# Token-major value and output-gate projections, with the lower halves of the weight splits made on GpSimd

## The chip, the cores and the metric

The kernel runs on one core of a Trainium2 chip. The metric is the device time of one execution in microseconds (us); the time given is the median of several executions. The engines are named as in the profile: PE (TensorE), DVE (VectorE), ACT (ScalarE), POOL (GpSimd) and SP (SyncE, which issues most DMAs). Each engine executes its own instructions in a fixed order and waits for others by semaphores.

## The reference

One layer of a hybrid trunk on 2048 latent tokens of width 1024, with 256 context tokens: a gated-linear-attention mixer (GLA, two directions, 4 heads) and a SwiGLU feed-forward network (FFN, width 2816). Only the latent stream is returned.

```python
D_MODEL = 1024; SEQ = 2048; CTX_LEN = 256; GLA_QK = 512; GLA_VD = 1024; GLA_RANK = 16; GLA_CHUNK = 64
mod_l = (silu(c) @ mod_w[i] + mod_b[i]).reshape(bsz, N_MOD, 1, D_MODEL)
h_lat = modulate(rms_norm(lat, norm_g[i, 0]), mod_l[:, 0], mod_l[:, 1])
...
z = h.astype(jnp.float32) @ w_in
q, k, v, r, glr = jnp.split(z, [GLA_QK, 2 * GLA_QK, 2 * GLA_QK + GLA_VD, 2 * GLA_QK + GLA_VD + D_MODEL], axis=-1)
g = log_sigmoid(einsum('blzr,zrk->blzk', glr, w_gate) + b_gate) / GLA_GATE_NORM
...
o_f, s_f = gla_chunk_scan(q, k, v, g_f, s_f0)
o_b, s_b = gla_chunk_scan(flip_seq(q), flip_seq(k), flip_seq(v), flip_seq(g_b), s_b0)
o = head_rms_norm(o_f + flip_seq(o_b), norm_g)
return (o * jax.nn.silu(r)) @ w_out, s_f, s_b
...
lat = lat + mod_l[:, 2] * rms_norm(y_lat, norm_g[i, 1])
h = modulate(rms_norm(lat, norm_g[i, 2]), mod_l[:, 3], mod_l[:, 4])
lat = lat + mod_l[:, 5] * rms_norm(swiglu(h, ffn_w_in[i], ffn_w_out[i]), norm_g[i, 3])
```

## The kernel before

Every large product of fp32 numbers is made of three matmuls of the faster type fp32r: both operands are split into an upper and a lower half, and `mm3` (L86 to L88) adds upper x upper, and upper x lower both ways. For activations and weights, `split` (L73 and L76) makes the upper half with a copy and the lower half with a subtraction on DVE.

The work has stages. First come the modulation vectors and the context tokens (256, to about 84 us in the profile), then four groups of 512 tokens, group 0 to group 3, to about 825 us. For a group, `make_h` transposes the normalised tokens (tp, on PE), scales and shifts them (hf, on ACT, L103) and splits them (hhi, hlo, on DVE), for k = 0 to 7, the eight pieces of 128 input channels. Then units of projection follow. A unit of `col_proj` holds a 128-column block of the weight still and streams 512 tokens: q, k and r. `proj_v` makes 256 columns of v for two tiles of 128 tokens, and `proj_vg` does so for the first 256 columns with the 32 columns of the low-rank gate (glr) behind them; its sums gs go through small DVE instructions and PE transposes (tpg) to glrS. `load_w` loads a weight piece of 128x1024 (wf, two buffers, 512 KB) and splits it into whi (ACT) and wlo (DVE), three buffers each. Projections write to PSUM in the banks pj (two), the transposes of make_h in the banks tp (two).

Between the units stand the stages s0 to s3 of the GLA chunks of 128 tokens of the same group or the one before: gates (pre, gcs, the scan cs), scores (sc, p), transposes of k (kt), the state Tf and the output o. In group 3 the chunk stages start with the 12th unit (`LAST_AT`), and its last three units (`tail`) are kept back. The modulation weights for later stages are summed on DVE (acc, L537) between the units of groups 1 and 2 (`mod_units`).

Phase 2 (860 to 1081 us) goes over the 16 chunks from the last to the first (`back`, b0 to b4): the state E of the backward scan, its output added to op, the norm of each head (on = op times rh), the transposes of on (tp2), the product with silu(r) (rt<-tp, L725), the split into ohi and olo, the output projection py with w_out (wo), the norm and the residual y (on POOL, L754). `load_wo` loads the eight pieces of wo before it, in the transition from 825 to 860 us, through two buffers (wof). Then the FFN follows, first product to 1937 us, second to the end.

The order on each engine is set when the kernel is built, by a scheduler that places instructions by their dependences and estimated times, from the order in which the code is written.

Of the kernel before, what the change touches and what calls it, by code (L numbers as in the profile page):

```python
# [34 lines left out]
def trunk(ctx, tc, x, cx, modw, cols, rows, consts, wqkr, wv, wvg, wgate, wout, w1, w2, out):  # L35
# [10 lines left out]
    r_d = [dram.tile([KT, 128, GT], F32, name=f"r_d{g}") for g in range(NG)]  # L46
# [83 lines left out]
    with tc.tile_pool(name="pro", bufs=1) as pro, tc.tile_pool(name="prop", bufs=1, space=PSUM) as prop:  # L130
# [64 lines left out]
    def make_h(xhs, nt, a):  # L195
# [42 lines left out]
    def col_proj(src, h, n, dst):  # L238
        whi, wlo = load_w(src, "", wp)
        ps = ps1.tile([128, 512], F32, name="pj", tag="pj", bufs=2)  # L240
# [3 lines left out]
        sb = hk.tile([128, GT], F32, name="stg", tag="stg", bufs=2)  # L244
# [23 lines left out]
    turns = []

    def proj_vg(h, g, tp, cache):  # L270
        if 0 not in cache or g == NG - 1:
            cache[0] = [load_vg(wvg[kh]) for kh in range(2)]
        pieces = cache[0]
        i = 1 if g == NG else g % 2
        sb = hk.tile([128, 2, 256], F32, name="stg", tag="stg", bufs=2)
        for t2 in range(2):
            t = 2 * tp + t2
            ps = ps1.tile([128, 512], F32, name="pj", tag="pj", bufs=2)
            for k in range(KT):
                whi, wlo = pieces[k // 4]  # L280
                hhi = h[0][k][:, 128 * t:128 * t + 128]
                hlo = h[1][k][:, 128 * t:128 * t + 128]
                ops = [(320, hhi, whi), (256, hhi, wlo), (288, hlo, whi)]
                if k == KT - 1:
                    ops = ops[1:] + ops[:1]
                for j, (n, a, w) in enumerate(ops):
                    nc.tensor.matmul(out=ps[:, 0:n], lhsT=a, rhs=w[:, k % 4, 0:n], start=(k == 0 and j == 0),  # L287
                                     stop=(k == KT - 1 and j == 2))
            evac(sb[:, t2, :], ps[:, 0:256])
            gs = hk.tile([128, 32], F32, name="gs", tag="gs", bufs=2)  # L290
            nc.vector.tensor_copy(out=gs, in_=ps[:, 288:320])
            nc.vector.tensor_add(out=gs, in0=ps[:, 256:288], in1=gs)  # L292
            nc.vector.tensor_copy(out=glt[2 * (tp % 2) + t2][:, 0:32], in_=gs)
            nc.vector.tensor_copy(out=glt[2 * (tp % 2) + t2][:, 64:96], in_=gs)
            nc.vector.tensor_sub(out=glt[2 * (tp % 2) + t2][:, 32:64], in0=gs, in1=glt[2 * (tp % 2) + t2][:, 0:32].bitcast(F32))
            st.dma_start(out=v_d[g][t, :, 0:256], in_=sb[:, t2, :])

        def turn():
            tps = ps1.tile([128, 512], F32, name="tpg", tag="tp", bufs=2)
            for t2 in range(2):  # L300
                nc.tensor.transpose(out=tps[:, 128 * t2:128 * t2 + 128], in_=glt[2 * (tp % 2) + t2].bitcast(F32), identity=ident)
            nc.vector.tensor_copy(out=glrS[i][:, 256 * tp:256 * tp + 256], in_=tps[:, 0:256])

        turns.append(turn)
# [49 lines left out]
    def gla_stages(g, i, c, first):  # L354
# [58 lines left out]
        def s2():  # L413
# [11 lines left out]
            for z in range(2):  # L425
# [74 lines left out]
    def proj_units(g, h, n):  # L500
# [10 lines left out]
        else:  # L511
# [3 lines left out]
            if g != NG:  # L515
                u += uq
# [710 lines left out]
```

## Time and profile before

| what | us |
| --- | --- |
| median of 3 runs | 2362.84 (2361.79 to 2365.46) |
| profiled execution | 2366.31 |
| its span, first to last instruction | 2364.5 |
| PE busy / DVE / ACT / POOL | 2301.9 / 1566.6 / 1066.5 / 328.4 |
| mean granted clock of TensorE | 0.991 of full speed |

Busy time of an engine is the time in which at least one of its instructions was under way. Matmuls overlap each other, so their mean durations are longer than the distance of their starts. [...] An engine that isn't the bottleneck may stand idle without cost.

### The profile page before, as it was taken

The page shows a single profiled execution, that of the slowest core. Times are in us where ns is not written, and L with a number is a line of the kernel's source. Part 1 is how long each engine was busy: PE and PEld are TensorE (multiplying, and loading weights), DVE is VectorE, ACT ScalarE, POOL GpSimd, SP SyncE. Part 2 cuts the span into 40 slices and gives each one's busy share as a digit, 9 for nine tenths or more (in the row PEclk, how much of TensorE's full clock was granted, in tenths as well). Part 3 has the DMA queues.
Part 4 walks back from the last instruction along what each step waited for, and adds up shares of the span by engine and source line. Part 5 has one row for each costly group of instructions (what it writes and reads, how often), then busy time and mean ns, then how long its engine had stood idle before and what let it go on. Part 6 is the DMA issues. An engine that isn't in the chain of part 4 may idle for free.

```text
span 2364.5 us, 32530 instructions
## 1 busy us (share of the span) xinstructions
PE 2301.9 (97%) x11546; PEld 1940.2 (82%) x11546; DVE 1566.6 (66%) x2462; ACT 1066.5 (45%) x1947; POOL 328.4 (14%) x513
## 2 busy tenths in 40 slices
PE   8999999999998999998999999999999999999998
PEld 4898898898898877776888888888888888888887
DVE  5756767666658586667866666876666657466554
ACT  3525435535546544336333333633333336555552
POOL 1100000000001023643511111111111110011001
PEclk9999999999999999999999999999999999999999
DMA  8765458465455587658633333743344348659655
GB/s 298 224 208 177 141 189 285 167 228 196 160 183 197 191 297 264 227 179 289 227 135 132 129 129 129 245 152 123 127 147 165 134 174 286 195 190 336 195 185 171
DMA packets 213254, 461.36 MB, mean 195 GB/s; under 512 B 22370, under 2 KB 66018, under 8 KB 213092
## 3 DMA queue, kind: packets, MB, share of 16 engines
q1 hardware_dynamic: 195188, 400.56, 50.3%
q0 software_dynamic: 17904, 58.73, 6.8%
q8 instruction: 90, 1.47, 0.3%
q14 instruction: 72, 0.59, 0.1%
HBM read 327.60 MB, written 131.60 MB: 194 GB/s over the span
## 4 chain that ended last, share of the span: by engine, by line
PE 75%; DVE 8%; DMA 6%; issue 5%; POOL 3%; ACT 3%; SPq 0%; POOLq 0%; DVEq 0%; ACTq 0%
PE X L964 19%; PE X L1111 10%; PE Z L964 10%; PE W L1111 8%; PE Y L964 5%; PE pj L87 5%; PE pj L86 5%; PE pj L88 5%; DMA xt<-modw 2%; POOL y L754 1%; PE o L494 1%; DMA xt<-x 1%; DVE cs L335 1%; PE sc L419 1%; PE pj L287 1%
## 5 line engine op out<-in xcount | busy, mean ns | idle before, releaser
L964 PE MATMUL X<-T,whl 128*128 128x512 f32 x2112 | 496.3, 390 | 5.2 <-ACT whl L946 2.1
L964 PEld LDWEIGHTS X<-T,whl 128*128 128x128 f32 x2112 | 397.6, 188 | 89.1 <-ACT whl L946 2.8
L964 PE MATMUL Z<-T,whl 128*128 128x512 f32 x1056 | 254.1, 389 | 1.8 <-ACT whl L946 1.8
L1111 PE MATMUL X<-wr,ar 128*128 128x512 f32 x1056 | 240.9, 389 | 0.0
L964 PEld LDWEIGHTS Z<-T,whl 128*128 128x128 f32 x1056 | 198.2, 188 | 43.2 <-ACT whl L946 2.2
L1111 PEld LDWEIGHTS X<-wr,ar 128*128 128x128 f32 x1056 | 198.2, 188 | 41.5
L86 PE MATMUL pj<-hhi,whi 128*128 128x512 f32 (+1 forms) x544 | 213.4, 395 | 2.1 <-DVE hhi L75 1.4
L87 PE MATMUL pj<-hlo,whi 128*128 128x512 f32 (+1 forms) x544 | 211.1, 388 | 0.0
L88 PE MATMUL pj<-hhi,wlo 128*128 128x512 f32 (+1 forms) x544 | 210.2, 387 | 0.0
L73 ACT CAST whi<-wf 128x1024 fp32r<-128x1024 f32 x104 | 109.0, 1048 | 194.4 <-PE pj L87 83.7
L1065 DVE TENSOR_TENSOR ar<-ar 128x512 fp32r<-128x512 f32 x154 | 106.0, 691 | 128.2 <-ACT ar L1064 127.7
L76 DVE TENSOR_TENSOR wlo<-wf,whi 128x1024 fp32r<-128x1024 f32 x104 | 126.8, 1220 | 87.3 <-ACT whi L73 81.8
L1111 PE MATMUL W<-wr,ar 128*128 128x512 f32 x792 | 180.8, 389 | 0.0
L1111 PEld LDWEIGHTS W<-wr,ar 128*128 128x128 f32 x792 | 148.7, 188 | 31.2
L1064 ACT CAST ar<-ar 128x512 fp32r<-128x512 f32 x154 | 95.5, 622 | 155.3 <-DMA ar<-S_d 120.1
L86 PE MATMUL pj<-whi,hhi 128*128 128x256 f32 x432 | 125.6, 291 | 5.9 <-DVE gs L292 4.9
L947 DVE TENSOR_TENSOR whl<-s,whl 128x512 fp32r<-128x512 f32 x132 | 98.2, 746 | 47.3 <-ACT whl L946 46.5
L964 PE MATMUL Y<-T,whl 128*128 128x512 f32 x528 | 127.6, 390 | 0.0
L87 PE MATMUL pj<-wlo,hhi 128*128 128x256 f32 x432 | 124.0, 287 | 2.9 <-DVE wlo L76 2.9
L88 PE MATMUL pj<-whi,hlo 128*128 128x256 f32 x432 | 123.4, 286 | 0.0
L87 PEld LDWEIGHTS pj<-hlo,whi 128*128 128x128 f32 x544 | 103.5, 190 | 21.2 <-DVE hlo L76 2.2
L86 PEld LDWEIGHTS pj<-hhi,whi 128*128 128x128 f32 x544 | 103.0, 190 | 21.4 <-DVE hhi L75 1.6
(234 smaller groups left out, 4428.6 us busy)
## 6 DMA issues: line engine op xcount, KB each, us to landing
ar<-S_d SPq DMA_DIRECT2D x154, 256.0 KB, 2.8
wf<-wqkr SPq DMA_DIRECT2D x68, 512.0 KB, 4.1
wg<-w SPq DMA_DIRECT2D x44, 512.0 KB, 3.8
wu<-w SPq DMA_DIRECT2D x88, 256.0 KB, 3.0
S_d<-sa POOLq DMA_DIRECT2D x88, 256.0 KB, 2.3
wr<-W_d SPq DMA_DIRECT2D x88, 256.0 KB, 2.9
wf<-wv SPq DMA_DIRECT2D x36, 512.0 KB, 4.0
S_d<-a POOLq DMA_DIRECT2D x66, 256.0 KB, 3.3
```

The lines of the kernel that those rows point to most:

```text
L73: nc.scalar.copy(out=hi, in_=src)
L76: nc.vector.tensor_sub(out=lo, in0=src, in1=hi.bitcast(F32))
L86: nc.tensor.matmul(out=ps, lhsT=ahi, rhs=bhi, start=start, stop=False)
L87: nc.tensor.matmul(out=ps, lhsT=ahi, rhs=blo, start=False, stop=False)
L88: nc.tensor.matmul(out=ps, lhsT=alo, rhs=bhi, start=False, stop=stop)
L287: nc.tensor.matmul(out=ps[:, 0:n], lhsT=a, rhs=w[:, k % 4, 0:n], start=(k == 0 and j == 0), stop=(k == KT - 1 and j == 2))
L335: nc.vector.tensor_tensor_scan(out=flat(cs[:, 4 * hh:4 * hh + 4, :]), data0=flat(rst), data1=flat(gcs), initial=0.0, op0=ALU.mult, op1=ALU ...
L947: nc.vector.tensor_sub(out=w[:, 1, :], in0=src, in1=w[:, 0, :].bitcast(F32))
L964: nc.tensor.matmul(out=ps, lhsT=w[:, a, ks], rhs=t[:, k, b, :], start=first and k == 0 and n == 0, stop=k == 3 and n == 2, skip_group_chec ...
L1064: nc.scalar.copy(out=t[:, 0, :], in_=raw)
L1065: nc.vector.tensor_sub(out=t[:, 1, :], in0=raw, in1=t[:, 0, :].bitcast(F32))
L1111: nc.tensor.matmul(out=po[j], lhsT=a[:, x, 128 * j:128 * j + 128], rhs=w[:, z, :], start=first and fp == 0 and n == 0, stop=fp == NFP - 1 ...
```

## The change

Projections: v and r are now made by `token_units`: for up to four tiles of 128 tokens a half of 512 columns at a time, each tile in a PSUM bank of its own, from four pieces of weight (each two k times 512 columns). In the context and in group 3 two tiles at a time. r is stored by token and no longer transposed. `proj_vg` is replaced by `glr_unit`: 16 matmuls against the gate's columns, a copy on ACT, six small DMAs that repeat the rows, and three DVE instructions. A piece's lower half is made by POOL, not by DVE. The number of pieces goes from 104 and 12 with the gate's columns to 124.

PSUM: four banks pj serve the units, make_h and the sums of mod_units; the buffers stg are four instead of two. A last sum of mod_units waits while a token unit has its banks open.

Order: make_h of group 0 stands behind all units of the context. In group 3 the gates of the first direction of chunks 0 and 1 are made two units and one unit ahead of `LAST_AT`. A kt that nobody used (second direction, chunk 0 of each sequence) is left out. The last three r units come ahead of all loads of wo.

Phase 2: silu(r) is multiplied in together with the head norm, before the transposes; ohi is a copy on ACT from PSUM, olo a subtraction on DVE that reads PSUM; the head norm's gain is multiplied into wo.

```diff
+    def load_w(src):
+        w = wp.tile([128, D], F32, name="wf", tag="wf", bufs=2)
         sync.dma_start(out=w, in_=src)
...
+        hi = wp.tile([128, D], F32R, name="whi", tag="whi", bufs=3)
+        lo = wp.tile([128, D], F32R, name="wlo", tag="wlo", bufs=3)
+        nc.scalar.copy(out=hi, in_=w)
+        nc.gpsimd.tensor_tensor(out=lo, in0=w, in1=hi.bitcast(F32), op=ALU.subtract)
         return hi, lo
...
+    def token_units(g, h, c, tiles, dst):
+
+        ps = []
+        step = 1 if len(tiles) == 4 else 2
+
+        def unit(p0):
+            held[0] = p0 + step < 4
+            if p0 == 0:
+                ps.extend(ps1.tile([128, 512], F32, name="pj", tag="pj", bufs=4) for t in tiles)
+            for p in range(p0, p0 + step):
+                whi, wlo = load_w(wvr[c, p])
+                for j, t in enumerate(tiles):
+                    for k2 in range(2):
+                        k, ks, ts = 2 * p + k2, slice(512 * k2, 512 * k2 + 512), slice(128 * t, 128 * t + 128)
+                        mm3(ps[j], h[0][k][:, ts], h[1][k][:, ts], whi[:, ks], wlo[:, ks], k == 0, k == KT - 1)
+                    if p == 3:
+                        sb = hk.tile([128, GT], F32, name="stg", tag="stg", bufs=4)
+                        evac(sb, ps[j])
+                        st.dma_start(out=dst(t), in_=sb)
...
+    def glr_unit(g, h, n):
         i = 1 if g == NG else g % 2
...
+        ps = ps1.tile([128, 512], F32, name="pj", tag="pj", bufs=4)
+        for k in range(KT):
+            nc.tensor.matmul(out=ps[0:64, 0:n], lhsT=wgs[:, k, :], rhs=h[0][k][:, 0:n], start=k == 0, stop=False,
+                             skip_group_check=True)
+            nc.tensor.matmul(out=ps[0:32, 0:n], lhsT=wgs[:, k, 0:32], rhs=h[1][k][:, 0:n], start=False, stop=k == KT - 1,
+                             skip_group_check=True)
+        g2, m, c = (hk.tile([128, GT], F32, name=x, tag="stg", bufs=4) for x in ("g2", "gm", "gc"))
+        nc.scalar.copy(out=g2[0:64, 0:n], in_=ps[0:64, 0:n])
+        for j in range(3):
+            sync.dma_start(out=m[32 * j:32 * j + 32, 0:n], in_=g2[0:32, 0:n])
+            sync.dma_start(out=c[32 * j:32 * j + 32, 0:n], in_=g2[32:64, 0:n])
+        nc.vector.tensor_add(out=m[0:96, 0:n], in0=m[0:96, 0:n], in1=c[0:96, 0:n])
+        nc.vector.tensor_copy(out=glrS[i][0:96, 0:n], in_=m[0:96, 0:n])
+        nc.vector.tensor_sub(out=glrS[i][32:64, 0:n], in0=m[32:64, 0:n], in1=glrS[i][32:64, 0:n].bitcast(F32))
...
-            transp_mod(ps1, "tp", 2, xhs, k, hf[:, 0:n], mcol[:, a, 1, k:k + 1], mcol[:, a, 0, k:k + 1])
+            transp_mod(ps1, "pj", 4, xhs, k, hf[:, 0:n], mcol[:, a, 1, k:k + 1], mcol[:, a, 0, k:k + 1])
...
+            v = [w for tp in range(2) for c in range(2) for w in v_units(c, (2 * tp, 2 * tp + 1))]
+            r = [w for tp in (1, 0) for c in (2, 3) for w in r_units(c, (2 * tp, 2 * tp + 1))]
...
-            hn = [make_h(norm_rows(x[0:GT, :], 4), 4, 0)]
...
+            xh0 = norm_rows(x[0:GT, :], 4)
             load_consts()
         u()
+    hn = [make_h(xh0, 4, 0)]
...
+                else:
+                    if stages:
+                        stages.pop(0)()
+                    if i + 1 in (LAST_AT - 2, LAST_AT - 1):
+                        gates(g, 0, i + 3 - LAST_AT)
...
-            split(w, *wo[k])
+            g = col[:, 96 + k % 2:97 + k % 2]
+            nc.scalar.activation(out=wo[k][0], in_=w, func=AF.Copy, scale=g)
+            nc.vector.scalar_tensor_tensor(out=wo[k][1], in0=w, scalar=g, in1=wo[k][0].bitcast(F32),
+                                           op0=ALU.mult, op1=ALU.subtract)
...
-                nc.vector.tensor_scalar_mul(out=on[:, h, :], in0=op[:, h, :], scalar1=rs[:, h:h + 1])
+                nc.vector.scalar_tensor_tensor(out=on[:, h, :], in0=op[:, h, :], scalar=rs[:, h:h + 1], in1=e["rt"][:, h, :],
+                                               op0=ALU.mult, op1=ALU.mult)
...
-                split(rt[:, ks, :], ohi[:, ks, :], olo[:, ks, :], "dve")
+                split(tp, ohi[:, ks, :], olo[:, ks, :])
```

What the edits move is seen in the order of the engines. On PE, the end of the context units, where make_h of group 0 (tp<-ident,xh, four transposes for each k) begins. Before, one k at a time between matmuls of the context's v:

```order
L88 MATMUL pj<-whi,hlo 128x256
L102 MATMUL tp<-ident,xh 128x128 x4
L86 MATMUL pj<-whi,hhi 128x256
L87 MATMUL pj<-wlo,hhi 128x256
L102 MATMUL tp<-ident,xh 128x128 x4
L88 MATMUL pj<-whi,hlo 128x256
```

Now all context units are done when it comes, and the first matmuls of group 0 (pj<-hhi,whi) stand right behind it; the gates of the first context chunk (pre) fall between the last of the transposes:

```order
L87 MATMUL pj<-wlo,hhi 128x512
L88 MATMUL pj<-whi,hlo 128x512
L102 MATMUL tp<-ident,xh 128x128 x20
L302 MATMUL pre<-glrS_377,wg_380 128x256 x2
L102 MATMUL tp<-ident,xh 128x128 x4
L302 MATMUL pre<-glrS_377,wg_380 128x256 x2
L302 MATMUL pre<-glrS_377,wg_381 128x256 x4
L102 MATMUL tp<-ident,xh 128x128 x8
L86 MATMUL pj<-hhi,whi 128x512
L87 MATMUL pj<-hlo,whi 128x512
```

The eight k have moved out of the cover of the context's matmuls. On POOL, the first chunk's copies of the scan (lnDf, lnDb) and the small steps of the norms (ma, ra). Before:

```order
L80 TENSOR_SCALAR ma<-ss 128x1
L82 TENSOR_TENSOR ra<-ma,nhalf 128x1
L342 COPY lnDf<-mid 128x4x2
L343 COPY lnDf<-cs_1046 128x4x2
L80 TENSOR_SCALAR ma<-ss 128x1
L82 TENSOR_TENSOR ra<-ma,nhalf 128x1
L342 COPY lnDb<-mid 128x4x2
L343 COPY lnDb<-cs_1070 128x4x2
L342 COPY lnDf<-mid 128x4x2
L343 COPY lnDf<-cs_1986 128x4x2
```

Now the splits of the weight pieces (wlo) stand in the same queue:

```order
L82 TENSOR_TENSOR ra<-ma,nhalf 128x1
L219 TENSOR_TENSOR wlo<-wf,whi 128x1024
L80 TENSOR_SCALAR ma<-ss 128x1
L82 TENSOR_TENSOR ra<-ma,nhalf 128x1
L318 COPY lnDb<-mid 128x4x2
L319 COPY lnDb<-cs_991 128x4x2
L80 TENSOR_SCALAR ma<-ss 128x1
L82 TENSOR_TENSOR ra<-ma,nhalf 128x1
L219 TENSOR_TENSOR wlo<-wf,whi 128x1024 x14
L318 COPY lnDf<-mid 128x4x2
L219 TENSOR_TENSOR wlo<-wf,whi 128x1024
L319 COPY lnDf<-cs_1699 128x4x2
```

A copy or a norm's step on POOL now waits for the splits ahead of it. On SP, the loads of wo (wof) and what is stored and loaded around them before:

```order
L672 DMA op_8331<-op_d_144 128x1024
L646 DMA wof<-wout 128x1024 x2
L660 DMA rt<-r_d_77 128x4x128
L246 DMA r_d_77<-stg 128x512
L668 DMA ub_8426<-ub_d_159 128x1024
L646 DMA wof<-wout 128x1024 x2
L670 DMA qb_8428<-qb_d_175 128x512
L672 DMA op_8430<-op_d_143 128x1024
```

And after:

```order
L641 DMA rt<-r_d_88 128x1024
L215 DMA wf<-wvr 128x1024
L628 DMA wof<-wout 128x1024 x2
L650 DMA ub_7656<-ub_d_170 128x1024
L652 DMA qb_7658<-qb_d_186 128x512
L654 DMA op_7660<-op_d_154 128x1024
L628 DMA wof<-wout 128x1024
L261 DMA r_d_86<-stg 128x512
L261 DMA r_d_87<-stg 128x512
L628 DMA wof<-wout 128x1024
```

The last weight piece of a projection (wf) now stands ahead of the first wof, and the stores of r from the last unit behind the third.

## Rows read from the trace of the kernel before

**Rows 1.** The page: the chain of waits that ended last.

```profile
PE 75%; DVE 8%; DMA 6%; issue 5%; POOL 3%; ACT 3%; SPq 0%; POOLq 0%; DVEq 0%; ACTq 0%
```

**Rows 2.** Windows by stage: length, busy time of each engine (instructions), clock, DMA.

```profile
35.00:84.00 49.00, 44.91 (x333) 42.79 (x333) 33.44 (x67) 24.38 (x35) 2.53 (x6) 0.94 0.69 223
...
620.00:825.00 205.00, 196.86 (x1233) 178.79 (x1232) 135.75 (x214) 115.83 (x208) 9.75 (x10) 0.98 0.52 180
...
860.00:1081.00 221.00, 210.26 (x993) 171.04 (x992) 145.76 (x276) 90.21 (x236) 102.96 (x130) 0.98 0.69 233
1081.00:1937.00 856.00, 846.94 (x3730) 700.31 (x3729) 595.75 (x902) 343.32 (x603) 144.45 (x242) 0.99 0.47 160
1937.00:2364.50 427.50, 420.26 (x1852) 347.13 (x1850) 252.23 (x374) 210.88 (x387) 26.39 (x53) 1.00 0.66 222
```

**Rows 3.** Waits of PE, projections: for whom, us in total, times, longest.

```profile
PE tp L102 <- ACT hf L103: 6.6, 6, 2.8
PE pj L86 <- DVE gs L292: 4.9, 2, 4.3
PE pj L87 <- DVE wlo L76: 2.9, 3, 2.1
...
PE pj L287 <- DVE whig L212: 2.4, 2, 1.4
```

**Rows 4.** Waits of PE, phase 2.

```profile
PE o L696 <- ACT hf L103: 3.9, 2, 3.2
...
PE tp L723 <- DVE on L704: 2.5, 1, 2.5
```

**Rows 5.** Windows at the start of group 3.

```profile
720.00:724.30 4.30, 0.00 (x0) 0.03 (x1) 4.28 (x8) 4.12 (x7) 1.27 (x2) 0.91 0.34 122
724.30:734.00 9.70, 8.40 (x37) 7.77 (x38) 9.70 (x24) 3.92 (x9) 1.96 (x2) 0.51 0.25 79
```

**Rows 6.** Timeline of PE at two places: start, length, instruction.

```profile
160.49 0.28 PE L88 MATMUL pj<-whi,hlo 128*128 128x256 f32 x1
160.61 0.28 PE L86 MATMUL pj<-whi,hhi 128*128 128x256 f32 x1
...
1117.40 2.88 PE L964 MATMUL Z<-T,whl 128*128 128x512 f32 x12
```

**Rows 7.** Groups of DVE instructions, 0 to 825 us: busy, mean ns, idle before.

```profile
L76 DVE TENSOR_TENSOR wlo<-wf,whi 128x1024 fp32r<-128x1024 f32 x104 | 126.8, 1220 | 87.3 <-ACT whi L73 81.8 <-PE sc L419 4.2 <-PE pj L548 1.2
...
L211 DVE TENSOR_TENSOR wlog<-wfg,whig 128x1024 fp32r<-128x1024 f32 x12 | 14.7, 1222 | 3.6 <-ACT whig L210 3.5
```

**Rows 8.** Single lines: count, ns shortest/median/longest, starts, form.

```profile
L754 POOL TENSOR_TENSOR y<-y,xt x15: 2338/2390/2792, 864.7 to 1077.8; 128x1024 f32<-128x1024 f32 x15
...
L75 DVE CAST ohi<-rt x32: 412/417/1659, 834.2 to 1066.3; 128x512 fp32r<-128x512 f32 x32
...
L684 DVE SCALAR_TENSOR_TENSOR E<-E,fb,ub x60: 467/475/2614, 819.2 to 1011.6; 128x256 f32<-128x256 f32 x60
...
L704 DVE TENSOR_SCALAR on<-op,rh x64: 341/349/2494, 827.9 to 1057.3; 128x256 f32<-128x256 f32 x64
...
L725 DVE SCALAR_TENSOR_TENSOR rt<-tp,col,rt x64: 469/475/484, 832.3 to 1065.3; 128x256 f32<-128x256 f32 x64
...
L342 POOL COPY lnDf<-mid x9: 194/1131/3481, 99.9 to 748.5; 128x8 f32<-128x8 f32 x9
```

**Rows 9.** The page's DMA issues (us to landing), and whi's line.

```profile
wf<-wqkr SPq DMA_DIRECT2D x68, 512.0 KB, 4.1
...
L73 ACT CAST whi<-wf x104: 1029/1049/1062, 28.5 to 807.1; 128x1024 fp32r<-128x1024 f32 x104
```

**Rows 10.** make_h: hf's line, and PE's timeline in group 2.

```profile
L103 ACT ACTIVATE hf<-tp,mcol x72: 547/775/797, 34.3 to 1101.7; 128x512 f32<-128x512 f32 x64, 128x256 f32<-128x256 f32 x8
...
432.59 0.66 PE L102 MATMUL tp<-ident,xh 128*128 128x128 f32 x4 [2.23 <-ACT hf L103]
```

**Rows 11.** The last wo_lo, from its line.

```profile
L76 DVE TENSOR_TENSOR wo_lo<-wof,wo_hi x8: 1211/1216/1226, 825.5 to 858.1; 128x1024 fp32r<-128x1024 f32 x8
```

More of the change, by code (lines that the diff above doesn't have):

```diff
@@ L34, in trunk @@
 @with_exitstack
-def trunk(ctx, tc, x, cx, modw, cols, rows, consts, wqkr, wv, wvg, wgate, wout, w1, w2, out):
+def trunk(ctx, tc, x, cx, modw, cols, rows, consts, wqk, wvr, wgl, wgate, wout, w1, w2, out):
     nc = tc.nc
@@ L45, in trunk @@
     v_d = [dram.tile([4, 128, D], F32, name=f"v_d{g}") for g in range(NG + 1)]
-    r_d = [dram.tile([KT, 128, GT], F32, name=f"r_d{g}") for g in range(NG)]
+    r_d = [dram.tile([128, D], F32, name=f"r_d{c}") for c in range(NC_)]
     T_d = [[dram.tile([4, 128, GT], F32, name=f"T_d{p}{i}") for i in range(7)] for p in range(2)]
@@ L238, in col_proj @@
     def col_proj(src, h, n, dst):
-        whi, wlo = load_w(src, "", wp)
-        ps = ps1.tile([128, 512], F32, name="pj", tag="pj", bufs=2)
+        whi, wlo = load_w(src)
+        ps = ps1.tile([128, 512], F32, name="pj", tag="pj", bufs=4)
         for k in range(KT):
@@ L268, in trunk @@
[L268 to L273, printed above, removed]
-        i = 1 if g == NG else g % 2
[L275 to L304, printed above, removed]
@@ new lines, in trunk @@
+    held = [False]
+    def token_units(g, h, c, tiles, dst):
[12 more added lines that the diff above has]
+                    if p == 3:
+                        sb = hk.tile([128, GT], F32, name="stg", tag="stg", bufs=4)
+                        evac(sb, ps[j])
+                        st.dma_start(out=dst(t), in_=sb)
+        return [lambda p0=p0: unit(p0) for p0 in range(0, 4, step)]
@@ L424, in s2 @@
             e["kt"] = []
-            for z in range(2):
+            for z in range(2 if gc else 1):
                 kt = gtile([128, H, 128], "kt")
@@ L443, in s3 @@
             vhi, vlo = e["vhi"], e["vlo"]
-            for z in range(2):
+            for z in range(len(e["kt"])):
                 khi, klo = e["kt"][z]
-                if z == 1 and gc == 0:
-                    break
                 if z == 1 and not (is_ctx and c == 0):
@@ L554, in finish @@
             else:
[L555 removed]
+                ps = ps1.tile([128, KT, 2], F32, name="pj", tag="pj", bufs=4)
                 for k in range(KT):
@@ L605, in trunk @@
                 extra[i]()
-            if mu and i >= 1:
-                mu.pop(0)()
+            if mu and i >= 1 and not (mu[0][0] and held[0]):
+                mu.pop(0)[1]()
             if is_last:
@@ L802, in trunk @@
     bk[0][0]()
-    load_wo(range(0, 4), c2, c2)
-    bk[0][5]((0,))
     tail[0]()
@@ L807, in trunk @@
     bk[1][0]()
-    bk[1][5]((0,))
     tail[1]()
-    bk[0][2]((0,))
     bk[1][1]()
-    for u in tail[2:]:
-        u()
-    bk[0][5]((1,))
-    bk[1][5]((1,))
+    tail[2]()
+    load_wo(range(0, 4), c2, c2)
     bk[2][0]()
```

152 lines of the change are left out of this document (52 added, 100 removed).

## The prediction

> **What bounds the kernel now.** I read the chain of waits first, then the busy time by stage, then what TensorE (PE) waited for in each stage. The chain is 75% PE [rows 1], so time is lost or won only where PE stands still or has more to do. The two FFN stages take 856 + 427.5 = 1283.5 us [rows 2]; the change edits no instruction in them, and I carry them over. What can move lies in the first 1081 us.
>
> There the waits of PE are few. In the projections it waited 6.6 us for hf (the scaled transposes in make_h), 4.9 us for gs (the gate sums of proj_vg), 2.9 us for wlo and 2.4 us for whig [rows 3]; in phase 2 it waited 3.9 us for hf and 2.5 us for on [rows 4]. [...]
>
> **The change part by part.**
>
> *Matmuls.* Two matmuls of 256 columns start 0.12 us apart, so two take 0.24 us; twelve of 512 columns took 2.88 us, the last one's 0.39 us included, which is (2.88 - 0.39) / 11 = 0.226 us each [rows 6]. The change removes 1296 matmuls of 256 (155.5 us) and 432 of proj_vg (256, 288 and 320 columns; at 0.13 us, a little over the 256's, 56.2 us), and adds 864 of 512 (195.3 us), 64 glr matmuls of 512 columns and 16 of 256 (16.4 us together); 18 transposes and 4 kt transposes go (an estimate of 0.1 us each, 2 us). Sum: **-2 us**. r keeps 768 matmuls of 512 columns, with the operands exchanged. The durations in the busy lists would tell another story, since matmuls overlap; the starts decide.
>
> *The splits on DVE.* 104 wlo splits of 1.22 us (126.8 us) and 12 wlog (14.7 us) leave DVE [rows 7], and with them the waits for wlo and whig, 2.9 + 2.4 us, and the lower clock behind the largest one (2.1 of the 2.9 us), which I put at 1 to 2 us: **-5 us** (0 to -7). Nothing is gained where DVE was only busy.
>
> *The splits on POOL.* The trace has no such instruction of POOL before 860 us. The nearest is the addition y of 128x1024 in phase 2: 2.34 to 2.79 us, median 2.39 [rows 8]; I take 2.4 us, and 124 of them are 298 us in some 790. What it does to DVE is the question. ohi takes 0.417 us and up to 1.66, E 0.475 and up to 2.61, on 0.349 and up to 2.49 [rows 8]: the long ones lie beside such a POOL instruction and end with it. Copies that read PSUM, rt<-tp, stay at 0.469 to 0.484 [rows 8]. The lock works the other way too: POOL's lnDf copy takes 0.19 us at best, 1.13 at the median and 3.48 at most [rows 8]. So each split holds up any DVE instruction that has all its inputs in SBUF. In the projections these are about 314 (36 scans, 28 acc, 36 ek, 32 eq, 40 hhi, 40 hlo, 18 vlo and others, counted from the program). POOL holds the lock 298/790 = 38% of the time; a DVE instruction that meets it waits half of 2.4 us: 314 x 0.38 x 1.2 = 143 us of DVE, an estimate, and as much as the 141.5 us taken away. DVE is then as late as before, at other places. The lower bound is no delay, if POOL waits instead; the upper one is all 143 us on DVE. PE feels little of that: before, with DVE as busy, it waited 10 us for it in the whole of [rows 3]. I take **+3 us** (0 to +12).
>
> [...]
>
> *Supply of pieces.* wf has two buffers. One turns over in landing (4.1 us), upper half on ACT (1.05) and lower half: 1.22 us on DVE before, 2.39 after [rows 7 to 9]. With about 0.5 us between steps that is 6.9 and 8.1 us for two pieces, 3.4 and 4.1 us each. A piece feeds 24 matmuls of 0.227 = 5.4 us in groups 0 to 2: no loss. In ctx and group 3 it feeds 12, 2.7 us. Group 3 has 8 pieces of 5.4 and 32 of 2.7, 131 us, in the 205 us from 620 to 825: 5.1 us a piece if the chunk work were spread evenly, which hides 4.1. It isn't: the last six pieces have none (at most 6 x 1.4 = 8 us). I take **+6 us** (0 to +15). In ctx 12 pieces need 12 x 4.1 = 49 us where they needed 41, which is why make_h of group 0 could hide between them; now it stands behind them. Its transposes then go at ACT's pace, 0.775 us for hf against 4 x 0.11 on PE [rows 10]: 8 x 0.33 = 2.7 us and the first wait. The stage lasted 49 us before; I take **+2 us** (-4 to +8).
>
> *make_h of groups 1 to 3.* All 8 k stand ahead of the first matmuls, in the same four banks as these. Group 2 did almost so before and waited 2.23 us there [rows 10], within the 6.6. I charge **+5 us** for three (0 to +9).
>
> *Start of group 3.* The gs that PE waited for at 720 stood on DVE behind four gate groups in a row. glr_unit makes no gs, and two of the gate groups now come one and two units earlier. [...] I take **-6 us** (0 to -9).
>
> *Transition.* The last r pieces come ahead of all wo loads. The first can be issued one turn of wf's buffers before the projections end at 825 [rows 2], near 820, and eight pieces in two buffers take four turns of 6.9 us (priced as wf before): the last is split near 848. The last wo_lo started at 858.1 before [rows 11]. So the loads are hardly later than they were; the first w_out matmuls are, and are covered by less: **+3 us** (0 to +6).
>
> *Phase 2.* Each chunk loses four rt<-tp (0.475) and two ohi (0.417 to 1.66) on DVE, and on turns into an instruction with two inputs (like E, 0.475). DVE's chain from the transposes to olo gets 2 to 3 us shorter, and two instructions less can meet POOL's y; ACT gets two casts (1.05 us for 1024 columns, so some 0.6 each). PE waited 2.5 + 3.9 us here [rows 4], with lower clock behind each; on itself is still held by y. **-5 us** (0 to -9).
>
> The rest I cost at nothing: the norm's gain in the wo splits (the same two instructions a piece, on the same engines), four stg buffers, r stored and loaded by chunk (as many bytes), and mod's last sums held while a token unit has its banks (two units at most, with nothing behind them before group 3). The cover of the last is the chunk work; without it they would cost the length of a unit once, some 5 us.
>
> Sum: -2 - 5 + 3 + 6 + 2 + 5 - 6 + 3 - 5 = +1 us on the span of 2364.5, in an execution of 2366.31 us. That execution lies 3.5 us above the median of 2362.84, so I forecast 2362.84 + 1 = **2364 us**.
>
> **The rivals.**
>
> *A, what I forecast:* the parts cancel. Its own range is -8 to +10 us, 2355 to 2373.
>
> *B, faster:* the waits of PE that DVE made go, and POOL's lock falls into time in which PE doesn't need DVE. Then -2 (matmuls) - 9 (start of group 3) - 7 (wlo and whig) - 9 (phase 2) + 2 (make_h) = -25 us, 2338. For it: in groups 0 to 2 PE waits for DVE so seldom that DVE has slack. Against it: ctx and group 3 have none.
>
> *C, slower:* the lock holds up POOL's splits themselves. DVE's longer instructions take 1.2 us; if one stands ahead of each split, a piece takes 4.1 + 0.6 = 4.7 us with two buffers. In group 3 that is 32 x (4.7 - 4.1) = 19 us, in ctx 12 x (4.7 - 3.4) = 16 us, less the 7 us of wlo and whig: +28 us, with half a clock behind each stall rather more, 2391. It decides as soon as a piece takes longer to make than the work that it feeds. The 3.48 us copy [rows 8] speaks for it; that a split waits ahead of time, with three buffers of whi and wlo, against it. [...]
>
> **How the numbers follow.** About 0.2% (4.7 us) is what can be told from no change. I give A 0.42, B 0.25 and C 0.33. Of A's range some two thirds lie within 4.7 us: same 0.27, and 0.07 faster and 0.08 slower. So faster 0.32, same 0.27, slower 0.41. The range goes to half of B and nearly to C: 2346 to 2388.
>
> **What the profile will show.** Right: POOL's splits at 2.4 us or more, and DVE's SBUF instructions (E, on; hlo, ek, eq and acc in the projections) with means above their undisturbed times; in the waits of PE, wlo comes back under POOL's name, in ctx and group 3, and gs and whig are gone; phase 2 is shorter than the 221 us of [rows 2]. Wrong: if PE doesn't wait for POOL at all (then B), if it waits in groups 0 to 2 (worse than C), if the stretch from 718 us on loses its lower clock entirely, or if the FFN stages change, which I held fixed.

## The result, and the profile after

The changed kernel takes 2407.39 us (median of 4 executions, 2403.67 to 2412.85) against 2364.15 us of the kernel before, run beside it: a ratio of 1.0172, 95% interval 1.0154 to 1.0190. It is 43 us slower. The forecast was 2364 us with a range of 2346 to 2388. "Slower" had the largest of the three chances, but the size and the mechanism were missed.

The head of the page after (span; busy us and share of the span of each engine):

```profile
span 2411.1 us, 30732 instructions
...
PE 2316.1 (96%) x10740; PEld 1908.4 (79%) x10740; DVE 1500.1 (62%) x2149; ACT 1090.0 (45%) x1984; POOL 628.3 (26%) x637
```

The windows of the changed kernel by stage: the context, groups 0, 1, 2, group 3 to the last projection, phase 2, and the first FFN product (length, busy time of each engine, clock, DMA):

```profile
35.00:95.00 60.00, 48.42 (x252) 40.09 (x252) 30.08 (x44) 26.05 (x37) 34.24 (x21) 0.87 0.65 205
95.00:257.00 162.00, 156.01 (x720) 129.06 (x721) 90.68 (x108) 71.99 (x115) 67.91 (x40) 0.96 0.54 180
257.00:448.00 191.00, 181.68 (x933) 153.11 (x932) 110.23 (x138) 90.13 (x157) 68.26 (x42) 0.99 0.57 190
448.00:640.00 192.00, 183.53 (x937) 154.83 (x937) 122.02 (x144) 89.93 (x154) 69.29 (x41) 0.98 0.62 206
640.00:886.00 246.00, 219.72 (x1149) 186.88 (x1148) 152.10 (x194) 135.30 (x238) 103.85 (x52) 0.94 0.56 191
886.00:1125.00 239.00, 231.64 (x1092) 188.22 (x1091) 127.39 (x220) 114.57 (x284) 104.70 (x132) 0.99 0.70 247
1125.00:1983.00 858.00, 846.27 (x3727) 699.64 (x3726) 596.71 (x898) 341.97 (x599) 144.69 (x242) 0.99 0.46 158
```

The kernel before took 49 us for the first of these [rows 2] and, from the same view of its trace, 158, 186 and 185 us for groups 0 to 2, and 220 + 249 = 469 us from there to the FFN:

```profile
84.00:242.00 158.00, 154.00 (x914) 137.61 (x913) 103.61 (x156) 73.89 (x119) 14.01 (x17) 0.99 0.59 196
242.00:428.00 186.00, 181.51 (x1116) 161.62 (x1115) 126.37 (x188) 88.16 (x153) 7.74 (x16) 1.00 0.65 216
428.00:613.00 185.00, 182.08 (x1116) 163.04 (x1115) 121.61 (x187) 88.53 (x154) 11.60 (x18) 0.99 0.56 190
```

After, it is 60, 162, 191, 192 and 246 + 239 = 485 us: 11, 4, 5, 7 and 16 us more. The loss lies in every stage of the projections. The FFN's first product takes 858 us against 856 [rows 2]; POOL's busy time in each of the groups 0 to 2 went from between 8 and 14 us to 68 or 69.

What PE waited for from 35 to 886 us (us in total, times, longest), the view of [rows 3]:

```profile
PE o L86 <- DVE Tf L435: 14.4, 5, 3.3
PE pj L87 <- POOL wlo L219: 11.9, 7, 5.3
PE tp L102 <- ACT hf L103: 8.4, 6, 2.0
PE pj L86 <- DVE stg L229: 5.7, 2, 4.2
PE pj L86 <- ACT hf L103: 4.4, 4, 2.3
...
PE U L86 <- DVE gcs L309: 3.8, 2, 2.2
PE U L86 <- DVE Tf L435: 2.8, 2, 1.5
```

The sums of proj_vg (gs, whig) are gone, as they must be; in their place PE waits for Tf, for wlo under POOL's name, and longer for hf and for copies of projections (stg). Before, it waited 2.7 us in all for Tf:

```profile
PE o L86 <- DVE Tf L461: 2.7, 2, 1.7
```

The places differ. In groups 0 to 2 PE waits for nothing that POOL makes, and 18.8 us for DVE; its 11.9 us for wlo lie in the context (4.6) and in group 3 (7.3). POOL's split is what it was priced at (ns shortest, median, longest):

```profile
L219 POOL TENSOR_TENSOR wlo<-wf,whi x124: 2345/2398/3591, 29.7 to 878.9; 128x1024 fp32r<-128x1024 f32 x124
```

DVE's instructions with two inputs in SBUF, in the projections (busy us, mean ns, idle before):

```profile
L311 DVE TENSOR_TENSOR_SCAN cs<-rst,gcs 128x516 f32<-128x516 f32 x36 | 54.4, 1511 | 0.9
...
L370 DVE SCALAR_TENSOR_TENSOR eq<-qc,eq 128x512 f32<-128x512 f32 x32 | 35.2, 1101 | 8.3 <-ACT eq L366 6.5 <-DMA qc<-q_d 1.8
...
L377 DVE TENSOR_TENSOR fz<-lnDf 128x4 f32<-128x4 f32 x17 | 20.1, 1183 | 4.4 <-POOL lnDf L319 2.9 <-ACT ts L416 0.9
...
L76 DVE TENSOR_TENSOR plo<-p,phi 128x512 fp32r<-128x512 f32 x16 | 15.3, 956 | 0.1
```

In the kernel before they took 1.23, 0.68, 0.16 and 0.68 us on the mean. One of the five waits for Tf, near the end of group 2, in the timelines of DVE, POOL and PE:

```profile
612.26 2.88 DVE L76 TENSOR_TENSOR plo<-p,phi 128x512 fp32r<-128x512 f32 x1
615.06 1.27 DVE L435 TENSOR_TENSOR Tf<-ts,U 128x512 f32<-128x512 f32 x2
```

```profile
612.21 2.38 POOL L219 TENSOR_TENSOR wlo<-wf,whi 128x1024 fp32r<-128x1024 f32 x1 [3.76 <-ACT whi L218]
```

```profile
613.60 0.28 PE L88 MATMUL U<-vhi,klo 128*128 128x256 f32 x1
615.79 0.48 PE L86 MATMUL o<-vhi,phi 128*128 128x256 f32 x1 [1.92 <-DVE Tf L435]
```

plo was ready to go at 612.26, 0.05 us after a split on POOL; it ends only at 615.14, half a microsecond behind the split, instead of at 612.94. Tf stands behind it on DVE, and PE's next matmuls need the PSUM bank that Tf reads: 1.92 us of nothing. And behind the stall the clock falls, as it did at the start of group 3 before [rows 5]:

```profile
615.70:622.00 6.30, 6.21 (x26) 5.53 (x27) 1.13 (x3) 2.16 (x4) 0.00 (x0) 0.73 0.52 163
```

0.73 of full speed on the mean of 6.3 us (0.50 in the windows of half a microsecond from 616.2 to 619.2 us, 1.00 in those from 619.7) is, as an estimate, another 6.3 x 0.27 = 1.7 us. The mean granted clock of the whole execution went from 0.991 to 0.982.

### The profile page after: what moved, and what is told of

It reads as the page before. It is cut to its first block, busy times and chain, and to the rows that moved or that the text cites. A ratio compares the mean times of both kernels' runs of the same rounds, so it can differ in the third digit from the quotient of the medians.

```text
span 2411.1 us, 30732 instructions
## 1 busy us (share of the span) xinstructions
PE 2316.1 (96%) x10740; PEld 1908.4 (79%) x10740; DVE 1500.1 (62%) x2149; ACT 1090.0 (45%) x1984; POOL 628.3 (26%) x637
## 4 chain that ended last, share of the span: by engine, by line
PE 52%; DMA 1%; DVE 1%; POOL 1%; ACT 1%; issue 1%; SPq 0%; POOLq 0%; ACTq 0%; DVEq 0%
PE X L934 19%; PE X L1081 10%; PE Z L934 9%; PE W L1081 7%; PE Y L934 5%; DMA T<-T_d 0%; POOL y L730 0%; DMA T_d<-hf 0%; DMA wg<-w 0%; DVE whl L917 0%; PE tp L102 0%; PE py L87 0%; PE py L86 0%; PE py L88 0%; DMA rt<-r_d 0%
## 5 line engine op out<-in xcount | busy, mean ns | idle before, releaser
L219 POOL TENSOR_TENSOR wlo<-wf,whi 128x1024 fp32r<-128x1024 f32 x124 | 308.3, 2488 | 403.9 <-ACT whi L218 389.9
L218 ACT CAST whi<-wf 128x1024 fp32r<-128x1024 f32 x124 | 129.9, 1048 | 223.4 <-PE pj L88 64.2
L87 PE MATMUL pj<-wlo,hhi 128*128 128x512 f32 x544 | 216.1, 397 | 11.9 <-POOL wlo L219 11.9
L86 PE MATMUL pj<-whi,hhi 128*128 128x512 f32 x544 | 218.8, 403 | 6.5 <-DVE stg L229 5.7
L88 PE MATMUL pj<-whi,hlo 128*128 128x512 f32 x544 | 215.3, 396 | 0.0
L962 POOL DMA_DIRECT2D S_d<-a x66 | 35.6, 540 | 458.1 <-DVE a L952 364.7
L87 PEld LDWEIGHTS pj<-wlo,hhi 128*128 128x128 f32 x544 | 104.2, 192 | 36.4 <-POOL wlo L219 15.4
L86 PEld LDWEIGHTS pj<-whi,hhi 128*128 128x128 f32 x544 | 104.0, 191 | 30.1 <-DVE stg L229 6.6
L88 PEld LDWEIGHTS pj<-whi,hlo 128*128 128x128 f32 x544 | 104.2, 191 | 22.2
L86 PE MATMUL pj<-hhi,whi 128*128 128x512 f32 (+1 forms) x288 | 112.4, 395 | 4.4 <-ACT hf L103 4.4
```

Of the source, the lines that this page charges most:

```text
L86: nc.tensor.matmul(out=ps, lhsT=ahi, rhs=bhi, start=start, stop=False)
L87: nc.tensor.matmul(out=ps, lhsT=ahi, rhs=blo, start=False, stop=False)
L88: nc.tensor.matmul(out=ps, lhsT=alo, rhs=bhi, start=False, stop=stop)
L218: nc.scalar.copy(out=hi, in_=w)
L219: nc.gpsimd.tensor_tensor(out=lo, in0=w, in1=hi.bitcast(F32), op=ALU.subtract)
L962: nc.gpsimd.dma_start(out=S_d[self.p][i][self.f % NFP], in_=t)
```

## The experiments

Each run was compared with the kernel before on the same chip; all ratios are to that kernel. "DVE's splits" below is the first run. Port theory, supply theory and structure theory are the three explanations that its expectation names. No run shows a port; what is meant, and what the runs can show, is that POOL's splits hold up DVE's instructions with SBUF inputs.

**The splits back on DVE**, all else as changed.

```diff
-        nc.gpsimd.tensor_tensor(out=lo, in0=w, in1=hi.bitcast(F32), op=ALU.subtract)
+        nc.vector.tensor_sub(out=lo, in0=w, in1=hi.bitcast(F32))
```

> The changed kernel with the lower halves of the weight pieces made on DVE again, all else as changed. Port theory (POOL's splits hold up DVE's instructions with SBUF inputs, and PE waits for Tf, eq and the scans): most of the 43 us come back, 2355 to 2375 us, and PE's wait for Tf falls from 14 us to under 5. Supply theory (a piece takes longer to make, so wf turns over more slowly): comes back too, 2360 to 2375, and above all in the context and in group 3. Structure theory (token units, make_h in one piece, banks and order cost the time, whoever makes the splits): stays at 2390 or above.

Measured: 2350.3 us, ratio 0.9928 (0.9904 to 0.9951). All of the loss came back and more: without POOL's splits the change is 18 us faster than the kernel before beside it (2368.48 us). The windows by stage (context, groups 0, 1, 2, group 3, phase 2), and PE's waits in the projections:

```profile
35.00:86.00 51.00, 45.20 (x253) 38.54 (x253) 32.72 (x57) 25.59 (x38) 2.85 (x6) 0.91 0.72 239
86.00:240.00 154.00, 151.82 (x720) 125.21 (x721) 101.06 (x133) 72.04 (x114) 17.25 (x18) 1.00 0.57 191
240.00:420.00 180.00, 179.14 (x935) 152.03 (x934) 117.25 (x159) 90.68 (x157) 11.99 (x16) 1.00 0.60 203
420.00:600.50 180.50, 178.96 (x932) 151.87 (x932) 124.37 (x168) 89.35 (x153) 10.64 (x16) 1.00 0.65 218
600.50:824.00 223.50, 213.68 (x1154) 182.54 (x1153) 160.37 (x232) 135.98 (x238) 11.28 (x14) 0.98 0.60 209
824.00:1068.00 244.00, 232.74 (x1090) 187.96 (x1088) 127.13 (x222) 115.34 (x285) 105.90 (x132) 0.99 0.68 242
```

```profile
PE tp L102 <- ACT hf L103: 3.4, 3, 1.9
PE pj L86 <- ACT hf L103: 2.8, 5, 1.0
PE pj L87 <- DVE wlo L219: 2.3, 5, 0.7
PE o L86 <- DVE Tf L435: 1.7, 2, 1.1
...
PE U L86 <- DVE Tf L435: 1.3, 1, 1.3
```

Structure theory falls. Port and supply theory both fit; the next runs part them.

**POOL busy for nobody, with DVE's splits.** For each piece POOL subtracts the upper half from itself, in two instructions of 128x512, into a scratch tile that nobody reads.

```diff
+        nc.vector.tensor_sub(out=lo, in0=w, in1=hi.bitcast(F32))
+        dm = wp.tile([128, 512], mybir.dt.bfloat16, name="dm", tag="dm", bufs=1)
+        for j in range(2):
+            hj = hi[:, 512 * j:512 * j + 512].bitcast(F32)
+            nc.gpsimd.tensor_tensor(out=dm, in0=hj, in1=hj, op=ALU.subtract)
```

> [...] Port theory: as slow as the changed kernel or slower, since DVE has its splits too: 2400 to 2430 us. Supply theory: as fast as with DVE's splits alone, within 6 us.

Measured: 2407.76 us, ratio 1.0170 (1.0150 to 1.0190): as slow as the change, though nothing reads POOL's result. DVE's own splits (1.22 us undisturbed) and scans (1.23) are held up, and PE waits for Tf again:

```profile
L219 DVE TENSOR_TENSOR wlo<-wf,whi 128x1024 fp32r<-128x1024 f32 x124 | 175.1, 1412 | 91.5 <-ACT whi L218 91.3
L315 DVE TENSOR_TENSOR_SCAN cs<-rst,gcs 128x516 f32<-128x516 f32 x36 | 49.4, 1371 | 0.6
```

```profile
PE o L86 <- DVE Tf L439: 11.0, 5, 3.5
...
PE pj L87 <- DVE wlo L219: 8.9, 10, 2.8
```

So the loss comes with POOL's instructions, whoever makes the pieces. The run doesn't free the pieces of POOL entirely: before it fills a buffer of whi again, ACT must wait until POOL has read it, and PE waited 2.6 us for whi and 8.9 us for DVE's wlo.

**Half of each split on POOL.**

```diff
+        nc.vector.tensor_sub(out=lo[:, 0:512], in0=w[:, 0:512], in1=hi[:, 0:512].bitcast(F32))
+        nc.gpsimd.tensor_tensor(out=lo[:, 512:1024], in0=w[:, 512:1024], in1=hi[:, 512:1024].bitcast(F32), op=ALU.subtract)
```

> The changed kernel with half of each lower half (512 columns) on DVE and the other half on POOL. [...] Port theory: half of the loss stays, 2380 to 2395 us. Supply theory: nearly all comes back, 2360 to 2372 us.

Measured: 2381.34 us, ratio 1.0059 (1.0040 to 1.0078). 31 of the 57 us between the change and DVE's splits remain: about half, as the port theory had it. The supply isn't quite restored here, though: POOL's half took 1.66 us on the mean, more than half of the change's 2.49, and PE waited 6.5 us for wlo (11.9 in the change, 2.3 with DVE's splits). By itself this run doesn't part the two theories.

**POOL's splits in the kernel before.**

```diff
-        split(w, hi, lo)
+        nc.scalar.copy(out=hi, in_=w)
+        nc.gpsimd.tensor_tensor(out=lo, in0=w, in1=hi.bitcast(F32), op=ALU.subtract)
```

> The kernel before, with its 104 wlo splits (not the 12 with the gate's columns) made by POOL, and nothing else changed. Port theory: slower by 20 to 45 us, 2385 to 2410, with PE waiting for Tf. Supply theory: slower by 5 to 20 us, in the context and in group 3. Structure theory: no change, within 5 us of 2364.

Measured: 2413.31 us, ratio 1.0193 (1.0170 to 1.0216), 45 us slower, a little over the range; PE waited 15.0 us for Tf. The one edit costs as much in the old structure as the whole change cost.

**A busy POOL that hardly reads.**

```diff
+        nc.vector.tensor_sub(out=lo, in0=w, in1=hi.bitcast(F32))
+        dm = wp.tile([128, 256], F32, name="dm", tag="dm", bufs=1)
+        nc.gpsimd.tensor_copy(out=dm[:, 0:1], in_=hi[:, 0:1].bitcast(F32))
+        for j in range(6):
+            nc.gpsimd.memset(dm, 0.0)
```

> As the run with DVE's splits, and for each piece POOL copies one column of the upper half (so that it comes at the piece's pace) and then fills a scratch tile of 128x256 six times, about as long as a split: POOL is as busy, but hardly reads SBUF. [...] If any busy POOL disturbs the others (its queue, power, writes): 2385 to 2410 us.

Measured: 2359.37 us, ratio 0.9967 (0.9954 to 0.9980), well below the 2385 of a POOL that disturbs merely by being busy. POOL was busy for more time than the change's 308 us of splits, and yet 48 of the 57 us are not there; DVE's instructions with two inputs in SBUF have their undisturbed means (casts and others with one input are a little longer: hhi 448 ns against 421):

```profile
L223 POOL MEMSET dm<- 128x256 f32 x744 | 238.2, 320 | 42.1
L221 POOL COPY dm<-whi 128x1 f32<-128x1 f32 x124 | 97.1, 783 | 313.6 <-ACT whi L218 311.6
```

```profile
L315 DVE TENSOR_TENSOR_SCAN cs<-rst,gcs 128x516 f32<-128x516 f32 x36 | 44.2, 1228 | 0.6
...
L374 DVE SCALAR_TENSOR_TENSOR eq<-qc,eq 128x512 f32<-128x512 f32 x32 | 21.9, 683 | 1.5 <-ACT khi L73 0.9 <-DMA qc<-q_d 0.5
```

So it is POOL's reading: fills of the same time in all leave these means where they were. The 9 us left over the run with DVE's splits can't be read from the profile, which is of the fastest execution (2351.9 us). The copies of one column do read, and take 783 ns on the mean, where a copy of eight columns takes 194 at best [rows 8]; whether they are the 9 us stays open.

One more rival can be put aside with these runs. The scheduler's order isn't the same in the change and with DVE's splits (94 of some 2150 other instructions of DVE stand elsewhere), so a worse order could have been the cause. But the runs with POOL busy for nobody and with the fills have, in their traces, the order of DVE's splits on DVE and ACT, and on PE too but for one transpose and one gate matmul that change places in the second. With the same order, POOL's reading costs the 57 us and POOL's fills 9.

**POOL's splits in groups 0 to 2 alone.**

```diff
+        who[0] = nc.vector if is_last else nc.gpsimd
...
+        who[0].tensor_tensor(out=lo, in0=w, in1=hi.bitcast(F32), op=ALU.subtract)
```

> The changed kernel with POOL's splits in groups 0 to 2 alone (72 of 124 pieces); the context and group 3 have theirs on DVE. If PE had slack there, as the prediction took it (3 us lost in groups 0 to 2), 2348 to 2358 us. If every split on POOL costs alike, 57 x 72/124 = 33 us over the run with DVE's splits: 2378 to 2390 us. Supply theory: as with DVE's splits, since a piece feeds 5.4 us there.

Measured: 2378.84 us, ratio 1.0052 (1.0036 to 1.0068): 28.5 us over DVE's splits, for 72 pieces, 0.40 us each; all 124 cost 57 us, 0.46 us each. PE waited for no piece of POOL's in this run, and longer for Tf than with DVE's splits (1.7 us there):

```profile
PE o L86 <- DVE Tf L437: 11.4, 4, 3.2
```

So PE has no slack for this in groups 0 to 2, and by its waits supply has no part in these 28.5 us.

**The splits in quarters.** Each of POOL's splits is made as four instructions of 256 columns.

```diff
+        for j in range(4):
+            js = slice(256 * j, 256 * j + 256)
+            nc.gpsimd.tensor_tensor(out=lo[:, js], in0=w[:, js], in1=hi[:, js].bitcast(F32), op=ALU.subtract)
```

> [...] If the loss is the length of one hold-up (DVE's instruction that PE waits for comes up to 2.4 us late): half or more comes back, 2370 to 2385 us. [...]

Measured: 2397.19 us, ratio 1.0113 (1.0085 to 1.0142), 12 us above the range. Its POOL group, and two waits of PE:

```profile
L221 POOL TENSOR_TENSOR wlo<-wf,whi 128x256 fp32r<-128x256 f32 x496 | 412.9, 863 | 319.8 <-ACT whi L218 319.4
```

```profile
PE pj L87 <- POOL wlo L221: 10.5, 13, 1.4
...
PE o L86 <- DVE Tf L437: 4.8, 3, 3.6
```

The wait for Tf fell from 14.4 to 4.8 us, so the length of one hold-up does count for it. But a piece now takes 4 x 0.86 = 3.5 us on POOL (an undisturbed quarter 0.74 at the median, so some took much longer; I had not priced that POOL gets slower too), and PE waits for wlo 13 times. The run doesn't cleanly part the length of one hold-up from the sum of them.

**Four buffers for rt**, with DVE's splits.

```diff
-            e["rt"] = sp.tile([128, H, DV], F32, name="rt", tag="rt", bufs=3)
+            e["rt"] = sp.tile([128, H, DV], F32, name="rt", tag="rt", bufs=4)
```

> As the run with DVE's splits, with four buffers for rt in phase 2 instead of three (ACT stood 6.7 us on a late load of rt there, and PE 4.2 us behind it). If that load is late for want of a buffer: 3 to 7 us faster, 2343 to 2347. If it is late on SP's queue for another reason: the same within 3 us.

Measured: 2348.43 us, ratio 0.9921 (0.9905 to 0.9937), not to be told from DVE's splits (0.9904 to 0.9951).

**y on DVE**, with DVE's splits and four buffers for rt.

```diff
-            (nc.vector if gc == 0 else nc.gpsimd).tensor_tensor(out=y, in0=y, in1=xt, op=ALU.add)
+            nc.vector.tensor_tensor(out=y, in0=y, in1=xt, op=ALU.add)
```

> As the run before it (four buffers for rt), and the addition y of phase 2 made by DVE instead of POOL. Port theory: y takes 1.2 us and not 2.4, E and on are no longer held by it, and PE's 3.1 us wait behind it for ohi goes: 3 to 10 us faster than that run. If DVE has no room in phase 2: as slow or slower.

Measured: 2338.20 us, ratio 0.9887 (0.9867 to 0.9907), 10 us faster than the run before it on the same chip. It beats both kernels. The group of y on POOL in the run without the edit, and on DVE with it:

```profile
L730 POOL TENSOR_TENSOR y<-y,xt 128x1024 f32<-128x1024 f32 x15 | 37.3, 2487 | 24.3 <-DVE y L728 19.3 <-DMA xt<-x 3.4 <-DMA rt<-r_d 1.6
```

```profile
L730 DVE TENSOR_TENSOR y<-y,xt 128x1024 f32<-128x1024 f32 x16 | 20.7, 1291 | 0.3
```

The windows of phase 2, from its first matmul with wo to the FFN's first matmul, without the edit and with it:

```profile
827.70:1066.20 238.50, 229.31 (x1087) 186.49 (x1085) 127.42 (x224) 116.53 (x288) 105.94 (x133) 0.99 0.70 249
```

```profile
826.00:1054.20 228.20, 225.22 (x1087) 186.20 (x1086) 144.13 (x238) 117.56 (x288) 71.60 (x119) 1.00 0.74 261
```

Of the 13.6 us between these two executions 10.3 lie there: PE stood idle for 9.2 us without the edit and for 3.0 with it, and the clock went from 0.99 to 1.00. y takes half as long; E is not faster for it (513 ns before the edit, 531 with it), so the part of the expectation that E would be released is wrong here. DVE waited less for the small norm steps that stand behind y on POOL, 37.3 against 21.2 us for the next norm's (rb). That speaks for the chain through y, but isn't shown to be the cause: the scheduler also gave DVE and PE another order in phase 2.

**y on DVE in the kernel before**, the same edit alone.

> The kernel before with the addition y of phase 2 on DVE instead of POOL, and nothing else changed. Port theory: y takes 1.2 us instead of 2.4 and no longer holds ohi, E and on: faster by 4 to 12 us, 2355 to 2362. If DVE's longer chain before the change (rt, ohi, olo) leaves no room: the same within 3 us.

Measured: 2353.87 us against 2369.42, ratio 0.9938 (0.9916 to 0.9959): 15.5 us faster (10 to 20 by the interval), a little more than expected. In this kernel the hold-up does go with it: E took 485 ns on the mean in phase 2 and not 563, on 349 and not 385, ohi 503 and not 611. How much of the gain is the hold-up, and how much y's shorter time, isn't parted.

**The subtractions ahead of the FFN on DVE too**, on top of y on DVE.

```diff
-                nc.gpsimd.tensor_tensor(out=out, in0=x, in1=y, op=ALU.subtract)
+                nc.vector.tensor_tensor(out=out, in0=x, in1=y, op=ALU.subtract)
...
-            nc.gpsimd.tensor_tensor(out=b[out], in0=b[x], in1=b[y], op=ALU.subtract)
+            nc.vector.tensor_tensor(out=b[out], in0=b[x], in1=b[y], op=ALU.subtract)
```

> As the run with y on DVE, and the 32 subtractions of 128x512 that POOL makes for the first FFN product (16 in phase 2, 16 at its start) on DVE too. Port theory: PE's waits at the start of the FFN get shorter, 2 to 8 us faster than that run, 2330 to 2336 us. If DVE has no room at the start of the FFN: the same or up to 5 us slower.

Measured: 2338.96 us, ratio 0.9872 (0.9848 to 0.9896): not to be told from the run with y alone (0.9867 to 0.9907). PE's waits at the start of the FFN didn't get shorter (3.2 us for xh and 1.2 us for whl in both), so POOL's subtractions weren't what they hang on.

## Why the prediction was wrong, step by step

**The step that failed** is the one on DVE's delay: "PE feels little of that: before, with DVE as busy, it waited 10 us for it in the whole of [rows 3]. I take +3 us (0 to +12)." POOL's splits cost 57 us in all (2407.39 against 2350.3 us). In groups 0 to 2 alone, where PE waits for nothing that POOL makes, they cost 28.5 us: this part of the term is already more than twice its upper bound.

The steps ahead of it came out nearly as they stand. POOL's split was priced at 2.4 us and took 2.398 at the median. The delay of DVE was estimated at 143 us. DVE's busy time other than wlo is 1500.1 us in the change and, from this row of the page with DVE's splits, 1526.7 - 151.3 (124 splits of 1.22 us) = 1375.4 us: a delay of 125 us.

```profile
PE 2295.1 (98%) x10740; PEld 1892.7 (81%) x10740; DVE 1526.7 (65%) x2273; ACT 1091.5 (46%) x1984; POOL 337.7 (14%) x513
```

What was wrong is the inference from DVE's busy time to PE's waits. First, the 10 us are the three waits for DVE that [rows 3] shows (gs, wlo, whig); the whole view has 18 us for DVE, and Tf, for which PE waited most after the change, is among the lines left out. Second, the 141.5 us of splits that left DVE and the 125 us of delay that came are not alike. A split is made ahead, for one of three buffers, and PE waited 2.9 us for all 104 wlo [rows 3]. The delay falls on whatever DVE has next: eq, plo, the scans, and behind them, in DVE's fixed order, Tf and the copies that free PSUM banks, for which PE waits at once. Equal delay isn't equal cost, either: with POOL busy for nobody DVE's busy time was 1616.2 us, 89.5 us more than with DVE's splits, and the loss was the same 57 us.

From 35 us to the last projection, PE's waits add up to 62 us in the change (to 886) and to 20 us with DVE's splits (to 824). The mean granted clock was 0.982 over a span of 2411.1 us against 0.993 over 2348.2: that is 43.4 - 16.4 = 27 us of lost clock more, an estimate. The two together come to a little more than the 62.9 us between these two spans, so they overlap. The clock falls behind the stall shown above; its share was worked out from the spans, not tried by itself.

**Splits off DVE (-5 us):** right as to whig, which is gone; wlo came back under POOL's name with 11.9 us. The lower clock in the term is in the trace of the kernel before: behind the 2.1 us wait for wlo it was 0.50 for 3.4 us, which is 1.7 us as an estimate.

**Supply (+6 us, 0 to +15):** not the main cause, and not far off in size. PE waits 9.6 us longer for wlo than with DVE's splits, all of it in the context and in group 3, where the prediction had put the term. How much of that is the longer turn of a piece stays open: with POOL busy for nobody, when DVE made the pieces, PE waited 8.9 us for them. Rival C, priced at 28 us, had the sign but not the mechanism: it needed each of POOL's splits to be held up by some 1.2 us, and they took 2.49 us on the mean against 2.34 at best; and it put the loss in the context and group 3, while groups 0 to 2 alone lose 28.5. The sign that the prediction gave for "worse than C", PE waiting for POOL in groups 0 to 2, didn't come: what POOL costs shows there as waits for DVE.

**The lock.** What the prediction calls a lock is in the traces a hold-up, and it falls on either engine. DVE's plo, begun 0.05 us after a split on POOL, took 2.88 us instead of 0.68 (above). POOL's copy of 3.48 us in [rows 8], of eight columns, ran beside three DVE instructions of 1.22 us in the kernel before and ended 0.05 us behind the third; undisturbed, such a copy took 0.19:

```profile
748.42 1.22 DVE L76 TENSOR_TENSOR wlo<-wf,whi 128x1024 fp32r<-128x1024 f32 x1
749.56 1.22 DVE L339 SCALAR_TENSOR_TENSOR cs<-cs,mid 128x1032 f32<-128x1032 f32 x1
750.70 1.22 DVE L76 TENSOR_TENSOR wlo<-wf,whi 128x1024 fp32r<-128x1024 f32 x1
```

```profile
748.49 3.48 POOL L342 COPY lnDf<-mid 128x8 f32<-128x8 f32 x1 [19.80 <-DVE fb L350]
```

The scans, of which no row before showed a hold-up, went from 1.228 to 1.511 us on the mean beside POOL's splits, and stayed at 1.228 beside its fills. By what the two engines hold each other up, no run shows.

**The rest of the change (matmuls, order of make_h, start of group 3, transition, phase 2):** without the two terms of POOL's splits and supply the sum was -8 us, and some -4 if wlo's part of the splits' term (2.9 us and its clock) goes too, since DVE has wlo in that run. With DVE's splits it measured -18 us against the kernel before in its own batch (2350.3 against 2368.48), so the rest was undervalued. The context and make_h of group 0 took 51 us against 49 (+2, as forecast); groups 0 to 2 gained 4, 6 and 4.5 us, where I had a loss for make_h; phase 2 and group 3 together gained 1.5 us, where I expected 8 (group 3, transition, phase 2). Single terms were not tried apart, and why groups 0 to 2 gained stays open. The 9 us that bound the term for the start of group 3 are the whole stall of [rows 5], an estimate: 4.3 us in which PE did nothing, and 9.7 us behind it at a clock of 0.51, 9.7 x 0.49 = 4.8 us. No run shows the 6 us taken of it; the clock in group 3 was 0.94 in the change and 0.98 with DVE's splits, as before [rows 2].

**Held fixed:** the FFN, rightly within 3 us.

## What to carry to other kernels

Before work is moved to an idle engine, ask what it does there to the busy one's instructions: here the subtractions that POOL made from SBUF took nearly as much of DVE's time as if DVE had made them (125 us against 151), at moments that nobody chose. Equal busy time is no measure: work that is made ahead into buffers can be late for free, while a delay strikes the urgent instructions and all that stands behind them in order. And where two explanations share a sign, a kernel that has one without the other (here POOL working for nobody) goes furthest towards parting them.

## What the runs showed that was not expected

A two-input DVE instruction of 4 columns (fz) took 0.16 us undisturbed and 1.18 us on the mean beside the splits. Eight of the 17 started 75 to 80 ns behind a split and took 2.33 us, as long as the split itself; the other nine took 0.13 to 0.16 us. So an instruction of 4 columns was held up by 2.17 us where plo, of 512, was by 2.20, and this one stood right behind a copy on POOL that a split followed. And the addition of 128x1024 that POOL had made all along cost the kernel before 15.5 us of 2369, though the waits of PE in phase 2 [rows 4] name it nowhere. The page's chain of waits by line does, with 1% of the span (POOL y L754), and I had not followed it there.
